# Modulation vectors after the first two chunks: products with a full row sum on TensorE, or scaling and summing on GpSimd with a last sum on TensorE

## The chip, the core and the metric

The kernel runs on one core of a Trainium2 chip. The core has TensorE (PE, matrix products into PSUM), VectorE (DVE), ScalarE (ACT) and GpSimd (POOL), each working through its own queue of instructions in order, and SyncE (SP), whose queue here issues the transfers of weights. ScalarE's queue issues transfers too. The metric is the device time of one execution in microseconds (us); a time of several executions is their median.

## What is computed

A block of two layers over 256 latent tokens and 256 context tokens with 1024 features. Each layer is modulated by six vectors of 1024 values for each of the two streams, cut from one product of a vector with a 1024 x 6144 matrix:

```python
c_act = jax.nn.silu(c)
cc_act = jax.nn.silu(c_ctx)
for l in range(DEPTH):
    sh1, sc1, g1, sh2, sc2, g2 = jnp.split((c_act @ w_mod[l] + b_mod[l])[:, None, :], 6, axis=-1)
    csh1, csc1, cg1, csh2, csc2, cg2 = jnp.split(cc_act @ w_mod[l] + b_mod[l], 6, axis=-1)
    y, yc = token_mixer(modulate(x, sh1, sc1), modulate(xc, csh1, csc1), ...)
    x = layer_norm(DEEPNORM_ALPHA * x + g1 * y, ln1_g[l], ln1_b[l])
    x = layer_norm(DEEPNORM_ALPHA * x + g2 * swiglu(modulate(x, sh2, sc2), ...), ln2_g[l], ln2_b[l])
    # the context stream the same with csh1 ... cg2, in the first layer only
```

`modulate` is a layer norm times (1 + scale) plus shift. The token mixer has a gated linear attention (GLA) with 4 heads, a differential attention with 8 heads and a latent attention (MLA) with 8 heads, merged by gates. The feed-forward part has 2816 hidden values. All inputs are float32.

## The kernel before

Weights come in tiles of up to 128 x 1024 values by a transfer on SP's queue into one of four buffers called raw (`load`, `fetch`, L181 to L196). Each half of a tile is split into a rounded part wh, by a copy on ScalarE (L212), and the rest wl, by a subtraction on VectorE (L213), and every product is made of three (`mm3`, L233): the lines L234, L235 and L236 are most of TensorE's work. Three tiles of wh and wl run ahead. The tile framework orders each engine's queue beforehand, by the priority that the order of the program gives and by what its plan takes for the times; on the chip each queue then runs strictly in that order.

The modulation vectors are made in pieces. Shift and scale of the first sub-layer of layer 0 are made at the start (`first_X`, `mod_first`, L277, closing product L318). All others stand in `mod_queue` (L334): four chunks of layer 0 and six of layer 1, each in two pieces of 512 columns, 20 pieces. A piece has four steps (`mod_step`, L289). A step loads 256 rows of 512 columns (L296) and makes eight small full-precision products (L299) whose stationary side is 32 columns of silu(c), two of them used; the four groups of 128 columns stand in four column groups of the array. After four steps ScalarE copies the sums (L304). `mod_close` (L309) brings them to columns by one product with a selector (L320), adds the bias (L325), halves the gates (L327), and, when a gate's chunk is whole, writes it to memory (L331) from 128 partitions, one value each. `gate_rows` (L354) later reads it back, spread over all partitions, by transfers on ScalarE's queue (L410).

What sets the place of the steps is `tick` (L338). It is called ahead of each weight tile, and every third call closes a finished piece and makes the next step. The last two pieces, the second gate of layer 1, are left out there; `mods_until` (L346) makes them in one go ahead of the last feed-forward part, and closes what is still open.

GpSimd does little: fills, and the power in `rpow` (L178), which every norm needs and which VectorE waits for (L702 and L795 in the heads, L381 in `modulate`), and a small product (L792). After the mixer, `load_cur` (L141, called at L1152) fetches the residual tokens on ScalarE's queue. The output projection keeps the last HELD column blocks of `w_out` from the first two token tiles for the other two (L1173).

Of the kernel before, what the change touches and what calls it, by code (L numbers as in the profile page):

```python
# [8 lines left out]
F32 = mybir.dt.float32  # L9
F32R = mybir.dt.float32r  # L10
AF = mybir.ActivationFunctionType
ALU = mybir.AluOpType
# [31 lines left out]
def hybrid_block_kernel(  # L44
# [18 lines left out]
    BUFS = dict(X=3, XL=3, A=3, Y=15, U=8, M=16, acc=8, a2r=2, a2=2, early=4, xt=2, raw0=11, raw1=5, u=27, wo=33, q=6, k=6, v=16, e=6, pT=11, rt=5, mr=3, mz=8, qr=2, rs=8, gt=6, o=3)  # L63
# [9 lines left out]
    HELD = 4  # L73
    FHELD = 1
    RND = 12
    PB = dict(mm=8, s=2, t=2, o=6, md=1, first=15)
# [13 lines left out]
    def keep(shape):  # L90
        """Columns of the store for what stays for the whole program."""
# [14 lines left out]
    def small(w=1):  # L106
        """w columns for values that are needed soon and briefly."""
        o = small_n[0]
        if o + w > SMALL:
            o = 0  # L110
        small_n[0] = o + w
        return ring[:, o:o + w]
# [8 lines left out]
    # the first transfers of a queue leave in the order given here  # L121
# [35 lines left out]
    # silu(c) and silu(c_ctx) as columns, the rest of the 32 columns zero  # L157
# [13 lines left out]

    mhalf = keep([P, 1])
    nc.gpsimd.memset(mhalf, -0.5)

    def rpow(o, v, a):
        """o = (v + a) ** -0.5 on a column."""
# [4 lines left out]
    def load(src, kt, n, tag=None):  # L181
        """[kt * 128, n] of a weight, at most 1024 values to a partition."""
# [5 lines left out]
    nfetch = [0]  # L188

    def fetch(raw, src, kt, n):  # L190
# [4 lines left out]
        nfetch[0] += 1  # L195
        return v  # L196

    def split(v, tag=None):
        """v [128, a, b] -> hi, lo as lists of a views [128, b]: products read them by k."""
# [21 lines left out]
    def wtiles(src, kt, cols):  # L221
        """Column ranges of a [kt * 128, .] weight side by side."""
# [15 lines left out]
    def feat_block(o, w, X, n0, n1, c0=0, m=P):  # L238
        """o[m, n] = sum_k w[k, c0:c0+m]^T X[k, n0:n1]"""
# [5 lines left out]
    def wfeat(src):  # L245
        """A [1024, 128] weight."""
# [3 lines left out]
    def wtok(src, tag=None):  # L250
        """A [1024, 256] weight as two halves of k."""
# [4 lines left out]
    def tok_block(o, ws, X, t0, c0, c1):  # L256
        """o[128 tokens, c1-c0] = X[:, t0:t0+128]^T w[:, c0:c1], k in order of ws"""
# [8 lines left out]
    # chunks of w_mod: 0 sh1, 1 sc1, 2 g1, 3 sh2, 4 sc2, 5 g2  # L266
# [5 lines left out]
    def mod_load(l, ch, pc, j, tag=None):  # L272
        """512 rows of 256 columns."""
# [3 lines left out]
    def mod_first(ch, pc, raws):  # L277
        """256 columns of a chunk of layer 0, both streams, by token; eight k tiles on four column groups."""
# [10 lines left out]
    def mod_step():  # L289
        """A quarter of a piece: 512 columns of a chunk, both streams, by token; each 128 have a column group."""  # L290
# [1023 lines left out]
```

## Time and profile before

| | before |
|---|---|
| device time, median of 3 runs | 2157.45 us (2156.32 to 2159.31) |
| span of the profiled execution, first to last instruction | 2154.1 us |
| TensorE busy | 2099.5 us, 97% |
| VectorE busy | 1436.7 us, 67% |
| ScalarE busy | 1076.6 us, 50% |
| GpSimd busy | 96.0 us, 4% |
| mean granted TensorE clock | 0.992 |

The span covers the profiled execution from its first to its last instruction; the times of the runs take in what lies around it as well. Busy times of TensorE (PE) are modelled at their ends, since its products overlap, so the distance from the start of one instruction to the start of the next is the better measure there. PEclk is the clock that TensorE was granted, as a part of full speed. A row of a group gives the line, the engine, the operation, the tiles written and read, the shapes and the number of instructions, then the busy time in us and the mean of one in ns, and then the engine's idle time ahead of them.

### The profile page before, as it was taken

The page shows a single profiled execution, that of the slowest core. Times are in us where ns is not written, and L with a number is a line of the kernel's source. Part 1 is how long each engine was busy: PE and PEld are TensorE (multiplying, and loading weights), DVE is VectorE, ACT ScalarE, POOL GpSimd, SP SyncE. Part 2 cuts the span into 40 slices and gives each one's busy share as a digit, 9 for nine tenths or more (in the row PEclk, how much of TensorE's full clock was granted, in tenths as well). Part 3 has the DMA queues.
Part 4 walks back from the last instruction along what each step waited for, and adds up shares of the span by engine and source line. Part 5 has one row for each costly group of instructions (what it writes and reads, how often), then busy time and mean ns, then how long its engine had stood idle before and what let it go on. Part 6 is the DMA issues. An engine that isn't in the chain of part 4 may idle for free.

```text
span 2154.1 us, 36382 instructions
## 1 busy us (share of the span) xinstructions
PE 2099.5 (97%) x14103; PEld 1812.2 (84%) x14103; DVE 1436.7 (67%) x3168; ACT 1076.6 (50%) x2495; POOL 96.0 (4%) x187
## 2 busy tenths in 40 slices
PE   7999999999999999999999999999999999998998
PEld 4888887777777778799899889988978888998998
DVE  5699657767467666685334448598566888785656
ACT  3756345666454553434231334765465676644452
POOL 0001001111000000010000000000000000000000
PEclk9999999999999999999999999999999999998999
DMA  9322343332322234627324446533434333568653
GB/s 294 102 87 69 118 99 93 86 106 60 91 81 66 78 127 137 176 84 214 104 89 127 118 127 182 159 91 118 136 88 128 106 113 85 172 191 213 172 178 116
DMA packets 349270, 268.29 MB, mean 125 GB/s; under 512 B 19932, under 2 KB 316520, under 8 KB 349096
## 3 DMA queue, kind: packets, MB, share of 16 engines
q1 hardware_dynamic: 335632, 252.22, 40.1%
q10 hardware_dynamic: 13464, 13.74, 2.1%
q8 instruction: 111, 1.82, 0.3%
q14 instruction: 63, 0.52, 0.1%
HBM read 263.79 MB, written 2.12 MB: 123 GB/s over the span
## 4 chain that ended last, share of the span: by engine, by line
PE 79%; DVE 11%; ACT 4%; issue 2%; POOL 2%; DMA 1%; ACTq 0%; DVEq 0%; POOLq 0%
PE ps_mm L234 18%; PE ps_mm L235 18%; PE ps_mm L236 18%; PE ps_s L234 3%; PE ps_s L236 3%; PE ps_s L235 3%; PE ps_s L509 3%; POOL store L178 2%; PE ps_s L508 2%; DVE wl L213 2%; PE ps_md L299 1%; PE ps_s L681 1%; DMA grow<-store 1%; ACT rt L483 1%; PE ps_t L928 1%
## 5 line engine op out<-in xcount | busy, mean ns | idle before, releaser
L213 DVE TENSOR_TENSOR wl<-raw,wh 128x512 fp32r<-128x512 f32 (+2 forms) x719 | 468.8, 674 | 139.7 <-ACT wh L212 82.4
L212 ACT CAST wh<-raw 128x512 fp32r<-128x512 f32 (+2 forms) x719 | 416.2, 611 | 254.1 <-PE ps_mm L235 135.0
L234 PE MATMUL ps_mm<-X,wh 128*128 128x512 f32 (+1 forms) x1264 | 440.8, 349 | 0.0
L235 PE MATMUL ps_mm<-XL,wh 128*128 128x512 f32 (+1 forms) x1264 | 437.4, 346 | 0.0
L236 PE MATMUL ps_mm<-X,wl 128*128 128x512 f32 (+1 forms) x1264 | 435.7, 345 | 0.0
L234 PEld LDWEIGHTS ps_mm<-X,wh 128*128 128x128 f32 x1264 | 241.2, 191 | 33.3 <-issue 7.3
L235 PEld LDWEIGHTS ps_mm<-XL,wh 128*128 128x128 f32 x1264 | 241.3, 191 | 27.3 <-issue 2.7
L236 PEld LDWEIGHTS ps_mm<-X,wl 128*128 128x128 f32 x1264 | 241.0, 191 | 26.2 <-issue 0.7
L236 PE MATMUL ps_mm<-wh,XL 128*128 128x256 f32 (+1 forms) x544 | 156.8, 292 | 0.0
L235 PE MATMUL ps_mm<-wl,X 128*128 128x256 f32 (+1 forms) x544 | 156.5, 292 | 0.1
L234 PE MATMUL ps_mm<-wh,X 128*128 128x256 f32 (+1 forms) x544 | 152.8, 294 | 0.0
L178 POOL TENSOR_TENSOR store<-store 128x1 f32<-128x1 f32 x112 | 75.6, 676 | 1657.4 <-DVE store L177 1633.9
L234 PE MATMUL ps_s<-X,wh 128*128 128x256 f32 (+1 forms) x384 | 126.2, 329 | 4.9 <-ACT wh L212 4.9
L236 PE MATMUL ps_mm<-wh,u 128*128 128x256 f32 x444 | 125.8, 283 | 0.0
L235 PE MATMUL ps_mm<-wl,u 128*128 128x256 f32 x444 | 125.6, 283 | 0.0
L234 PE MATMUL ps_mm<-wh,u 128*128 128x256 f32 x444 | 125.6, 283 | 0.0
L236 PE MATMUL ps_s<-X,wl 128*128 128x256 f32 (+1 forms) x384 | 125.1, 326 | 0.0
L235 PE MATMUL ps_s<-XL,wh 128*128 128x256 f32 (+1 forms) x384 | 125.0, 326 | 0.0
L234 PE MATMUL ps_mm<-Y,wh 128*128 128x512 f32 (+1 forms) x352 | 119.9, 341 | 0.1
L235 PE MATMUL ps_mm<-Y,wh 128*128 128x512 f32 (+1 forms) x352 | 118.6, 337 | 0.0
L236 PE MATMUL ps_mm<-Y,wl 128*128 128x512 f32 (+1 forms) x352 | 118.4, 336 | 0.0
L723 ACT ACTIVATE e<-ps_s,store 128x512 f32<-128x512 f32 (+1 forms) x144 | 88.5, 617 | 47.1 <-DVE store L721 45.4
(306 smaller groups left out, 4481.7 us busy)
## 6 DMA issues: line engine op xcount, KB each, us to landing
raw<-in_w_in_dram SPq DMA_DIRECT2D x144, 512.0 KB, 4.6
raw<-in_w_mod_dram SPq DMA_DIRECT2D x96, 512.0 KB, 3.7
raw<-in_ffn_w_in_dram SPq DMA_DIRECT2D x96, 512.0 KB, 7.1
raw<-in_w_branch_dram SPq DMA_DIRECT2D x48, 512.0 KB, 3.5
raw<-in_ffn_w_out_dram SPq DMA_DIRECT2D x46, 512.0 KB, 3.4
raw<-in_w_out_dram SPq DMA_DIRECT2D x16, 512.0 KB, 4.2
raw<-in_w_in_dram SPq DMA_DIRECT2D x16, 448.0 KB, 3.4
v<-grow ACTq DMA_DIRECT2D x12, 256.0 KB, 4.1
```

Source lines behind the costliest of these rows:

```text
L178: nc.gpsimd.tensor_tensor(o, o, mhalf, op=ALU.pow)
L212: nc.scalar.copy(h, v[:, o:o + step, :])
L213: tt(lo, v[:, o:o + step, :], r32(h), op=ALU.subtract)
L234: mm(o, lh, rh, start=start, stop=False)
L235: mm(o, lh, rl, start=False, stop=False)
L236: mm(o, ll, rh, start=False, stop=stop)
L299: mm(pm[32 * g:32 * g + 32, :], cst[:, 2 * j + k, :], v[:, k, P * g:P * g + P], start=(j == 0 and k == 0), stop=(j == 3 and k == 1))
L483: act(qw[a:a + 32, :], pl[b:b + 32, :], AF.Copy, scale=f)
L508: mm(o, qs[m][:, q], ks[m][:, k], start=start, stop=False)
L509: mm(o, qs[2][ROWS[m], q], ks[m][ROWS[m], k], start=False, stop=stop)
L681: mm(pa[:, i, :], kx[:, P * i:P * i + P], qx[:, P * j:P * j + P], start=True, stop=True)
L723: act(e, pscore, AF.Exp, bias=mx, accum_out=s)
```

## The change

The pieces in `mod_queue` are no longer multiplied on TensorE. `mod_step` loads the same rows into tiles of their own (mraw, three of them), placed on SP's queue behind the weight load last issued. For each of the two row tiles and each stream GpSimd scales the 128 x 512 weights by a column of silu(c) and adds the result to an accumulator (macc). Both streams are made only where both are used: in layer 0 and in the first two chunks of layer 1. `mod_close` then sums over partitions on TensorE. For shifts and scales that is a product of each 128 columns with a column of ones; for gates it is a product of a constant 128x128 tile of 0.5 with the 512 columns, whose first row, with half of the bias row (fetched on ScalarE's queue), is written to memory as one piece of 512 values. The PSUM bank of the old sums goes. Two more edits: HELD is 3 instead of 4, and the transfers of `load_cur` stand on ScalarE's queue behind the last rounding copy that the program issued ahead of the last gate blocks. In the diff, edits that take away comments alone are left out.

```diff
-    BUFS = dict(..., mr=3, ...)
+    BUFS = dict(..., mr=4, mraw=3, macc=6, mt=1, ...)
-    HELD = 4
+    HELD = 3
-    PB = dict(mm=8, s=2, t=2, o=6, md=1, first=15)
+    PB = dict(mm=8, s=2, t=2, o=6, first=15)
+    halves = keep([P, P])
+    nc.gpsimd.memset(halves, 0.5)
 def fetch(raw, src, kt, n):
...
+    seen["load"] = getattr(ins, "ins", ins)
 def mod_step():
+    l, ch, pc = mod_queue[0]
     if not mod_now:
-        mod_now.extend([0, ps("md", [P, P])])
-    j, pm = mod_now
-    l, ch, pc = mod_queue[0]
+        n = 2 if l < DEPTH - 1 or ch < 2 else 1
+        mod_now.extend([0, [T([P, 512], "macc") for _ in range(n)]])
+    j, sums = mod_now
     c0 = ch * D + 512 * pc
-    v = load(w_mod[l, 256 * j:256 * j + 256, c0:c0 + 512], 2, 512)
+    with tc.issue_after(seen["load"]):
+        v = load(w_mod[l, 256 * j:256 * j + 256, c0:c0 + 512], 2, 512, "mraw")
     for k in range(2):
-        for g in range(4):
-            mm(pm[32 * g:32 * g + 32, :], cst[:, 2 * j + k, :], v[:, k, P * g:P * g + P],
-               start=(j == 0 and k == 0), stop=(j == 3 and k == 1))
+        for s, a in enumerate(sums):
+            c, fresh = cst[:, 2 * j + k, s:s + 1], j == 0 and k == 0
+            t = a if fresh else v[:, k, :] if s == len(sums) - 1 else T([P, 512], "mt")
+            nc.gpsimd.tensor_scalar(t, v[:, k, :], c, None, op0=ALU.mult)
+            if not fresh:
+                nc.gpsimd.tensor_tensor(a, a, t, op=ALU.add)
     mod_now[0] += 1
     if j == 3:
-        row = T([P, 512], "mr")[:, 0:P]
-        nc.scalar.copy(row, pm)
-        mod_open.append((l, ch, 4 * pc, 4, row))
+        mod_open.append((l, ch, 4 * pc, 4, sums))
 def mod_close():
-    l, ch, k0, nk, row = mod_open.pop(0)
+    l, ch, k0, nk, sums = mod_open.pop(0)
+    if ch in (2, 5):
+        if (l, ch) not in grow:
+            grow[l, ch] = tc.dram_tile([2, D], F32, name=f"grow{l}_{ch}")
+        br = T([P, 512], "mr")[0:1, :]
+        nc.scalar.dma_start(br, b_mod[l:l + 1, ch * D + P * k0:ch * D + P * k0 + 512])
+        for s, a in enumerate(sums):
+            pt = ps("mm", [P, 512])
+            mm(pt, halves, a, start=True, stop=True)
+            row = T([P, 512], "mr")[0:1, :]
+            stt(row, br, 0.5, pt[0:1, :], op0=ALU.mult, op1=ALU.add)
+            nc.scalar.dma_start(grow[l, ch][s:s + 1, P * k0:P * k0 + 512], row)
+        return
...
-        mm(pt, row, sel[:, 2:10], start=True, stop=True)
+        ns = len(sums)
+        for q in range(nk):
+            for s, a in enumerate(sums):
+                mm(pt[:, ns * q + s:ns * q + s + 1], a[:, P * q:P * q + P], scan1[:, 0:1], start=True, stop=True)
...
-    if ch in (2, 5):
-        ts(o, o, 0.5, None, op0=ALU.mult)
-        if k0 + nk == KD:
-            d = tc.dram_tile([2, D], F32, name=f"grow{l}_{ch}")
-            for s in range(2 if l < DEPTH - 1 else 1):
-                nc.scalar.dma_start(d[s].rearrange("(k p) -> p k", p=P), mc[:, :, s])
-            grow[l, ch] = d
 def hilo(src, hi, lo, f=None):
     if f is None:
-        nc.scalar.copy(hi, src)
+        ins = nc.scalar.copy(hi, src)
+        seen["act"] = getattr(ins, "ins", ins)
...
+    heads_done = seen["act"]
     XM = [pair("M", TQ) for n in range(KD)]
     gates(2, range(8))
     G1, B1 = bcast_row(ln1_g[l], "e"), bcast_row(ln1_b[l], "e")
-    load_cur(NT)
+    with tc.issue_after(heads_done):
+        load_cur(NT)
```

## Rows read from the trace of the kernel before

**Rows 1.** The page: busy us, share of the span and instructions of each engine.

```profile
PE 2099.5 (97%) x14103; PEld 1812.2 (84%) x14103; DVE 1436.7 (67%) x3168; ACT 1076.6 (50%) x2495; POOL 96.0 (4%) x187
```

**Rows 2.** Busy time by stretch: from:to, length, each engine (instructions), PEclk, DMA share, GB/s.

```profile
323.10:646.20 323.10, 317.33 (x1797) 245.34 (x1797) 221.54 (x535) 187.68 (x504) 34.70 (x70) 1.00 0.29 86
861.60:915.50 53.90, 48.64 (x301) 40.98 (x299) 34.75 (x62) 23.26 (x42) 0.00 (x0) 0.94 0.65 176
107.70:215.40 107.70, 103.57 (x643) 88.23 (x642) 102.19 (x230) 62.40 (x138) 9.25 (x16) 1.00 0.25 78
1400.10:1454.00 53.90, 52.05 (x385) 47.44 (x385) 52.61 (x157) 33.31 (x89) 1.68 (x6) 1.00 0.32 91
1938.60:1992.50 53.90, 45.71 (x361) 43.98 (x361) 30.74 (x62) 22.80 (x51) 0.55 (x1) 0.84 0.89 213
```

**Rows 3.** Stretches again, the instructions of L299 alone: PE and PEld busy, PEclk, DMA.

```profile
107.70:215.40 107.70, 1.93 (x48) 1.13 (x48) 1.00 0.25 78
323.10:646.20 323.10, 11.23 (x224) 5.86 (x224) 1.00 0.29 86
1400.10:1454.00 53.90, 1.89 (x34) 1.08 (x34) 1.00 0.32 91
1930.00:1945.00 15.00, 3.91 (x118) 3.09 (x122) 0.91 0.65 189
```

**Rows 4.** Timeline of TensorE, four places: start us, us, line, tiles, count, [idle before].

```profile
18.23 0.61 PE L318 MATMUL ps_mm<-store,mr 128*128 128x2 f32 x4
...
221.71 0.39 PE L235 MATMUL ps_mm<-XL,wh 128*128 128x512 f32 x1
221.94 0.39 PE L236 MATMUL ps_mm<-X,wl 128*128 128x512 f32 x1
222.26 0.64 PE L299 MATMUL ps_md<-raw,store 128*32 128x128 f32 x16
222.83 0.50 PE L234 MATMUL ps_mm<-X,wh 128*128 128x512 f32 x1
...
882.63 0.28 PE L320 MATMUL ps_mm<-store,mr 128*128 128x8 f32 x2
882.84 0.64 PE L299 MATMUL ps_md<-raw,store 128*32 128x128 f32 x16
...
1963.55 0.58 PE L234 MATMUL ps_s<-X,wh 128*128 128x256 f32 x1 [2.96 <-ACT wh L212]
```

**Rows 5.** Groups of TensorE by line and shape: the closing products of the start.

```profile
L318 PE MATMUL ps_mm<-store,mr 128*128 128x2 f32 x32 | 4.6, 248 | 0.5 <-ACT mr L284 0.5
```

**Rows 6.** The chain that ended last, its longest pieces: start us, us, what.

```profile
253.18 1.73 PE ps_s L630 x8
...
1951.37 11.11 DMA grow<-store
```

**Rows 7.** Groups of GpSimd by line and shape.

```profile
L178 POOL TENSOR_TENSOR store<-store 128x1 f32<-128x1 f32 x112 | 75.6, 676 | 1657.4 <-DVE store L177 1633.9 <-DVE store L614 23.2
L792 POOL TENSOR_SCALAR store<-store 128x1 f32<-128x1 f32 x48 | 16.6, 345 | 301.7 <-ACT e L723 301.5
L525 POOL MEMSET a2r<- 96x512 f32 x4 | 2.0, 522 | 43.1 <-DVE XL L471 43.1
L155 POOL MEMSET store<- 128x256 f32 x1 | 0.3, 312 | 0.3 <-POOLq L1298 0.3
```

**Rows 8.** Timeline of VectorE and GpSimd at two places.

```profile
332.28 0.41 DVE L485 SCALAR_TENSOR_TENSOR rt<-ps_mm,store 128x256 f32<-128x256 f32 x1
...
332.44 0.55 POOL L178 TENSOR_TENSOR store<-store 128x1 f32<-128x1 f32 x1 [0.58 <-DVE store L177]
...
1578.10 0.68 DVE L213 TENSOR_TENSOR wl<-raw,wh 128x512 fp32r<-128x512 f32 x1
...
1578.26 0.93 POOL L178 TENSOR_TENSOR store<-store 128x1 f32<-128x1 f32 x1 [1.91 <-DVE store L177]
```

**Rows 9.** Waits of the whole span: who for whom, us in total, times, longest.

```profile
DVE o L795 <- POOL store L178: 13.2, 32, 0.7
```

More of the change, by code (lines that the diff above doesn't have):

```diff
@@ L61, in nm @@
         return f"{s}_{uid[0]}"
-    BUFS = dict(X=3, XL=3, A=3, Y=15, U=8, M=16, acc=8, a2r=2, a2=2, early=4, xt=2, raw0=11, raw1=5, u=27, wo=33, q=6, k=6, v=16, e=6, pT=11, rt=5, mr=3, mz=8, qr=2, rs=8, gt=6, o=3)
+    BUFS = dict(X=3, XL=3, A=3, Y=15, U=8, M=16, acc=8, a2r=2, a2=2, early=4, xt=2, raw0=11, raw1=5, u=27, wo=33, q=6, k=6, v=16, e=6, pT=11, rt=5, mr=4, mraw=3, macc=6, mt=1, mz=8, qr=2, rs=8, gt=6, o=3)
     def T(shape, tag, dtype=F32):
@@ L188, in hybrid_block_kernel @@
     nfetch = [0]
+    seen = {}
     def fetch(raw, src, kt, n):
@@ L314, in mod_close @@
         mc = mcols[l, ch]
+        ns = 2
         pt = ps("mm", [P, 2 * nk])
@@ L317, in mod_close @@
             for q in range(2):
-                mm(pt[:, 2 * q:2 * q + 2], row[:, P * q:P * q + P], sel[:, 0:2], start=True, stop=True)
+                mm(pt[:, 2 * q:2 * q + 2], sums[:, P * q:P * q + P], sel[:, 0:2], start=True, stop=True)
         else:
-            mm(pt, row, sel[:, 2:10], start=True, stop=True)
+            ns = len(sums)
+            for q in range(nk):
+                for s, a in enumerate(sums):
+                    mm(pt[:, ns * q + s:ns * q + s + 1], a[:, P * q:P * q + P], scan1[:, 0:1], start=True, stop=True)
         b0 = 48 * l + 8 * ch + k0
-        bias = bcol[:, b0:b0 + nk].rearrange("p (q o) -> p q o", o=1).to_broadcast([P, nk, 2])
-        o = mc[:, k0:k0 + nk, :]
-        p3 = pt.rearrange("p (q s) -> p q s", s=2)
-        stt(o, p3, 1.0 if ch in (1, 4) else 0.0, bias, op0=ALU.add, op1=ALU.add)
-        if ch in (2, 5):
-            ts(o, o, 0.5, None, op0=ALU.mult)
-            if k0 + nk == KD:
-                d = tc.dram_tile([2, D], F32, name=f"grow{l}_{ch}")
-                for s in range(2 if l < DEPTH - 1 else 1):
-                    nc.scalar.dma_start(d[s].rearrange("(k p) -> p k", p=P), mc[:, :, s])
-                grow[l, ch] = d
+        bias = bcol[:, b0:b0 + nk].rearrange("p (q o) -> p q o", o=1).to_broadcast([P, nk, ns])
+        p3 = pt[:, 0:ns * nk].rearrange("p (q s) -> p q s", s=ns)
+        stt(mc[:, k0:k0 + nk, 0:ns], p3, 1.0 if ch in (1, 4) else 0.0, bias, op0=ALU.add, op1=ALU.add)
     mod_queue = [(l, ch, pc) for l in range(DEPTH) for ch in range(6) for pc in range(2) if l or ch > 1]
```

## The prediction

> **What bounds the kernel now.** I read the busy totals of the page first: TensorE is busy 97% of the span, VectorE 67%, ScalarE 50%, GpSimd 4% [rows 1]. So whatever leaves TensorE's stream is time, as long as nothing else takes its place, and GpSimd has room. Then I split the span into stretches [rows 2]. Three kinds of stretch matter. In the first GLA heads of layer 0 (107.7 to 215.4 us) VectorE is busy 102.2 of 107.7 us and TensorE 103.6: both are full. At the start of layer 1's GLA heads (1400.1 to 1454.0) VectorE is busy 52.6 of 53.9. In the differential-attention part of layer 0 (323.1 to 646.2) VectorE has 101 us idle. Two stretches, around 890 and 1960 us, have an idle TensorE and a granted clock of 0.94 and 0.84; what stops it there is told below. The stretches by the line of the old modulation products, L299, show where a quarter-piece ("step") falls: 16 instructions are one step, so 48, 224, 34 and 118 instructions are 3, 14, about 2 and about 7 steps [rows 3].
>
> **What is taken off TensorE.** 20 pieces of four steps make 80 steps; a step is 16 instructions of L299 [rows 4]. One step starts at 222.26 us and the next product at 222.83: 0.57 us. The product ahead of it lasted 0.32 us to the step's start, where an ordinary one takes 0.23 (221.71 to 221.94), so another 0.09 [rows 4]. 80 x 0.66 = 53 us. The closing product L320 takes 882.63 to 882.84, 0.21 us [rows 4], 20 x 0.21 = 4 us. Together 57 us. Seven of the steps run from 1930 to 1945 us [rows 3], a burst while TensorE waits for the residual and layer norm anyway; 7 x 0.66 = 5 us of it is no gain. Gain: 52 us.
>
> **What is put on TensorE.** A close of a shift or scale piece now takes one full-precision product with a 128x128 stationary and a single moving column for each 128 columns and stream: 8 pieces with two streams (8 products each) and 4 with one (4 products), 80 products. A product is two instructions, as L318 shows: four of them take 0.61 us, and one alone 0.248, so (0.61 - 0.25) / 3 = 0.12 us from start to start [rows 4, 5]. 80 x 2 x 0.12 = 19 us. A close of a gate piece is one product of 512 moving columns for each stream: 4 pieces with two and 4 with one, 12 products, 24 instructions. Eight instructions of 256 columns take 1.73 us [rows 6], 0.216 each, so 0.43 for 512: 24 x 0.43 = 10 us. Added: 29 us. Net off TensorE: 52 - 29 = 23 us.
>
> **The gate rows' way through memory.** Today a finished gate chunk is written as single elements from 128 partitions (L331), and the write takes 11.1 us at 1951.37 [rows 6]; one more such write stands in the chain, as long, in the stretch from 861.6 us. ScalarE's queue holds the read of it (L410) next, so ScalarE stops, then the weight casts, then TensorE. For the later one that is 2.96 us of TensorE's waiting [rows 4], and a share of the clock: the stretch has 8.2 us of idle TensorE, and its clock of 0.84 (a part of it at the lower level, 1.2 GHz) costs 0.16 x 53.9 = 8.6 us [rows 2]; 2.96 of 8.2 idle makes 3.1 of it. For the earlier one, TensorE is idle 53.9 - 48.6 = 5.3 us, and 0.06 of 53.9 us, 3.2 us, goes with the clock [rows 2]. The new rows are written as 2 KB in one piece by partition 0. If ScalarE no longer stops there, 6.1 + 8.5 = 14.6 us come back; bounds 0 (the row now comes later and stops the same queue) and 15. I take 14: nothing else of the chain in those stretches is as long as the write. So the two gains make 37 us.
>
> **What GpSimd now does.** 12 pieces with two streams have 16 scalings and 14 sums, 8 with one stream half that: 256 scalings and 224 sums of 128x512. The trace has no such operation, only narrow ones and fills. A fill of 512 columns takes 0.522 us and one of 256 takes 0.312 [rows 7], 0.82 ns a column. A scaling of one column takes 0.345 us [rows 7]; with 511 more columns 0.345 + 0.42 = 0.76. A sum reads two operands: 0.76 if side by side, 0.345 + 0.84 = 1.18 if in turn, 0.676 + 0.84 = 1.51 at L178's base [rows 7]. I take 1.18, the middle. A step with two streams is 4 x 0.76 + 4 x 1.18 = 7.8 us, with one 3.9; in all 256 x 0.76 + 224 x 1.18 = 459 us, 21% of the span. A close comes a tick later: three weight loads of 24 products at 0.23 us, 16 us, in layer 0 and half that in layer 1. So in the ticked stretches sums are in time and TensorE doesn't wait; in a backlog it could, 0 to 30 us (the last burst's 8 steps x 3.9), taken as 0. The Trainium skill ("GPSIMD Engine Reference", section "Performance versus the Vector engine") gives about 2.6 cycles per element for a two-input operation on GpSimd; by it a sum would take about 1.1 us, an estimate, and the total 441 us; no run here has yet shown one.
>
> **What that costs beside it.** First the read port. L178 takes 0.55 us when VectorE is at L485, which reads PSUM and one operand of SBUF, but 0.93 when L213, with two SBUF operands, is running: it ends 0.41 us after L213 does [rows 8]. So GpSimd waits out a VectorE instruction of two SBUF operands. The other direction, VectorE waiting for a wide GpSimd operation, has no row, since GpSimd's reads are one column today. The bounds are 0 and the whole read, 0.42 us for a scaling and 0.84 for a sum: 5.0 us a step with two streams, 2.5 with one, 256 x 0.42 + 224 x 0.84 = 296 us in all. I take the whole read, times the chance that VectorE wants the port. The Trainium skill ("SBUF — State Buffer", section "Who interferes with whom") calls it an exclusive lock, held for the whole instruction, the later one blocked; for GpSimd as the later one the trace agrees (0.93 against 0.55).
> In the first GLA stretch, 3 steps x 5.0 x 0.9 = 13.5 us less 5.5 idle is 8 us; at 1400 us, 2 x 2.5 x 0.95 = 4.8 less 1.3 is 3. In the differential heads 14 x 5.0 = 70 us, half of it met, 35 us against 101 us of idle VectorE; as it falls in chains of softmax and norm, I take a quarter, 9 us (0 to 35). In the feed-forward parts it is hidden by VectorE's idle time: 0.
> Second, the power L178 now queues behind modulation on GpSimd; VectorE's L795, L702 and L381 wait for it, and behind them on VectorE stand the weight splits L213. Today that wait is 13.2 us in 32 times at L795 [rows 9]. GpSimd would be busy 14 x 7.8 = 109 of 323 us, a chance of 0.34; 40 powers x 0.34 x 0.9 us (one operation on average) = 12 us, a quarter of it on the path, 3, and 1 in layer 1 (0 to 16). Third, the residual stage at 1930 to 1945: three powers and the two-operand L984 beside the last burst, 3 us (0 to 12). Fourth, HELD 3 loads and splits one w_out block again: 4 x 0.68 us (L213 [rows 8]) on VectorE, 1 us (0 to 3).
> Edits at no cost: loads of w_mod queue on SP behind the last weight load and wait there for GpSimd to free one of three tiles, so weight loads stand behind them; the four weight buffers cover that, which w_mod no longer shares. If GpSimd falls a whole step behind, 7.8 us, cover is gone and ScalarE's casts and TensorE wait for the rest. The late load_cur on ScalarE's queue is hidden by eight gate blocks, 8 x 24 x 0.23 = 44 us. The fill of the new constant lies in the start.
> Sum of the costs: 11 + 9 + 4 + 3 + 1 = 28 us.
>
> **How the numbers follow.** 2154.1 - 37 + 28 = 2145.1 us of span. The median of the runs, 2157.45, is 3.35 above the span, so 2148.5 us, 0.4% faster. A difference under 0.2%, 4.3 us, can hardly be told from none.
> Forecast, gain partly eaten, 2130 to 2153 us: chance 0.33.
> Rival A, VectorE's idle time hides nearly all: costs of 5 to 9 us, 2157.45 - 37 + 8 = 2128, down to 2115 if the free weight buffers give TensorE a little more. For it: VectorE is idle for a third of the span [rows 1]. Chance 0.16.
> Rival B, no change: costs of 33 to 41 us, or TensorE's columns go but its operands come no sooner (the change doesn't do what it says; only the gate rows' 14 us are left against some 12 of cost): 2153 to 2161. Chance 0.14.
> Rival C, slower: the port. VectorE's two-operand instructions wait for GpSimd's reads in the attention heads as well, and the in-order VectorE hands that on to the weight splits and the softmax. It decides when more than 37 of the 296 us, one eighth, reach the end; at a fifth, 59 us, it is 2157.45 - 37 + 59 = 2179, at a quarter 2194. For it: [rows 8] and a full VectorE in the GLA stretches; against it: the idle third elsewhere, and the feed-forward parts, which take their share of the steps. Chance 0.37. By the Trainium skill's lock ("SBUF — State Buffer", same section) this is the rival to expect when both engines are busy; its mechanism here is worked out above from rows.
> Faster 0.33 + 0.16 = 0.49, same 0.14, slower 0.37. The range of 2115 to 2194 takes in A, the forecast, B and C up to a quarter; the forecast's own is 2130 to 2153.
>
> **What would show it.** Right: L299 gone, the closes near 29 us, no wait for a grow write over 3 us, GpSimd busy 450 to 600 us with sums near 1.2 us. Right on the port: L213 longer than 0.68 us beside a wide GpSimd operation, and more VectorE time in the GLA stretches. Wrong: waits of TensorE on GpSimd at the closes, waits of VectorE on L178 far over 20 us, or SP waiting for GpSimd ahead of weight loads; then C's price is too low.

## The result and the profile after

The change makes the kernel slower: 2341.38 us (median of 4 runs, 2334.76 to 2345.84) against 2157.07 us in the same session, a ratio of 1.0853 with an interval of 1.084 to 1.0865. The forecast was 2148.5 us, the range ended at 2194. The profiled execution of after has a span of 2341.9 us, 188 us above the one of before.

The page first: its span, and busy us, share and instructions by engine (compare [rows 1]).

```profile
span 2341.9 us, 35242 instructions
PE 2124.9 (91%) x12967; PEld 1835.0 (78%) x12967; DVE 1589.1 (68%) x3168; ACT 1104.1 (47%) x2479; POOL 865.6 (37%) x668
```

TensorE has 1136 products fewer and is busy longer. GpSimd went from 96 to 866 us, and VectorE, which has the same number of instructions, from 1437 to 1589: the same work takes it 152 us more.

Where the time went is read best by stage. I cut each trace at the same products: the first of the GLA heads, the first scores of the differential heads, the last transposition of these heads, the first product with w_out, the first with w_ffn_out's operand (`ps_mm<-wh,u`), the last of layer 0's `ps_mm<-wo,u` (the stage called norms begins there), and so on for layer 1. The lengths, in us, with the experiments told below:

| stage | before | after | norms off GpSimd | scaling on ScalarE | sums filled | fills | narrow |
|---|---|---|---|---|---|---|---|
| start | 66.9 | 68.1 | 72.8 | 70.8 | 69.8 | 82.2 | 69.0 |
| GLA heads, layer 0 | 248.1 | 278.5 | 277.8 | 272.0 | 264.7 | 248.9 | 249.5 |
| differential heads, layer 0 | 302.8 | 373.8 | 307.4 | 313.3 | 340.0 | 305.3 | 306.4 |
| MLA heads and gates, layer 0 | 277.3 | 296.1 | 297.0 | 282.9 | 321.9 | 290.2 | 285.6 |
| w_out, residual, first feed-forward, layer 0 | 202.8 | 220.6 | 196.4 | 205.6 | 216.9 | 187.3 | 182.9 |
| feed-forward, layer 0 | 219.8 | 216.5 | 216.5 | 216.5 | 216.6 | 216.6 | 216.5 |
| norms to layer 1 | 59.4 | 64.9 | 63.0 | 68.2 | 65.2 | 59.1 | 59.1 |
| GLA heads, layer 1 | 188.8 | 206.4 | 197.4 | 198.3 | 190.9 | 185.4 | 185.5 |
| differential heads, layer 1 | 206.9 | 212.6 | 210.8 | 213.0 | 211.7 | 207.6 | 207.4 |
| MLA heads, layer 1 | 137.5 | 139.4 | 138.9 | 139.4 | 139.4 | 138.9 | 138.9 |
| w_out, residual, first feed-forward, layer 1 | 172.7 | 194.0 | 195.6 | 178.9 | 188.4 | 176.2 | 169.3 |
| feed-forward, layer 1 | 71.1 | 71.0 | 71.2 | 71.1 | 71.1 | 71.1 | 71.2 |

The feed-forward part of layer 0 is the only stage that gained (3.3 us). The largest loss, 71 us, is in the differential heads of layer 0, then 30 us in its GLA heads, 18 to 21 us in each of four others. Here are the first two, before and then after, and three others of after (columns as in [rows 2]).

```profile
66.90:315.00 248.10, 243.86 (x1542) 209.67 (x1540) 191.17 (x395) 141.11 (x295) 11.57 (x22) 1.00 0.32 94
315.00:617.80 302.80, 297.03 (x1688) 227.16 (x1687) 207.52 (x508) 174.27 (x480) 35.75 (x72) 1.00 0.31 89
```

```profile
68.10:346.60 278.50, 250.74 (x1384) 213.08 (x1385) 225.37 (x395) 142.48 (x295) 143.27 (x105) 0.96 0.26 77
346.60:720.40 373.80, 315.03 (x1504) 242.01 (x1503) 222.80 (x509) 176.43 (x478) 180.43 (x170) 0.90 0.24 71
1016.50:1237.10 220.60, 191.98 (x1189) 175.54 (x1188) 131.98 (x233) 71.42 (x141) 148.87 (x96) 0.93 0.38 114
1237.10:1453.60 216.50, 216.50 (x1374) 197.21 (x1373) 112.09 (x189) 63.69 (x106) 47.79 (x32) 1.00 0.39 121
2076.90:2270.90 194.00, 161.69 (x1271) 157.89 (x1271) 123.81 (x229) 78.11 (x161) 51.58 (x34) 0.90 0.56 161
```

The two stages lose in different ways. In the GLA heads VectorE runs the same 395 instructions for 225.4 instead of 191.2 us: 34 us more, against 30 us of stage. In the differential heads VectorE grows by only 15 us, but the stage by 71: TensorE stands idle for 373.8 - 315.0 = 58.8 us where it was 5.8. The granted clock is 0.90 there, some of it at the lower of the two levels (1.2 GHz), after stretches in which TensorE was idle. Its 1504 products take 315 us; the 1504 of the kernel called narrow below take 291.9 us at 1.00, so the clock costs about 23 us on top of the waits.

GpSimd's groups (form of [rows 7]) show what the added operations cost.

```profile
L308 POOL TENSOR_SCALAR mraw<-mraw,store 128x512 f32<-128x512 f32 x140 | 261.1, 1868 | 138.7 <-DMA mraw<-in_w_mod_dram 138.3 <-DVE rt L1177 0.3
L310 POOL TENSOR_TENSOR macc<-macc,mraw 128x512 f32<-128x512 f32 x140 | 190.3, 1359 | 6.2
L308 POOL TENSOR_SCALAR mt<-mraw,store 128x512 f32<-128x512 f32 x84 | 153.0, 1822 | 292.8 <-DMA mraw<-in_w_mod_dram 256.8 <-PE ps_mm L239 35.8
L310 POOL TENSOR_TENSOR macc<-macc,mt 128x512 f32<-128x512 f32 x84 | 118.3, 1409 | 3.8
L180 POOL TENSOR_TENSOR store<-store 128x1 f32<-128x1 f32 x112 | 73.5, 658 | 542.0 <-DVE store L179 535.0 <-DVE store L631 6.7
L308 POOL TENSOR_SCALAR macc<-mraw,store 128x512 f32<-128x512 f32 x32 | 58.0, 1820 | 315.8 <-DVE wo L217 145.4 <-DMA mraw<-in_w_mod_dram 125.1 <-DVE U L981 33.1
```

A scaling (L308) takes 1.82 to 1.87 us on the mean, a sum (L310) 1.36 to 1.41; together 780.7 us. Undisturbed they take 1.56 and 1.26 us, about the shortest of the trace. The row of L180 has the other half of the story: GpSimd sat idle for 535 us waiting for VectorE to hand it the input of a power, with its next scalings queued behind.

The waits of after, engine by engine (form of [rows 9]), have VectorE waiting for those same powers.

```profile
DVE o L812 <- POOL store L180: 44.1, 37, 5.2
DVE rs L850 <- POOL store L180: 30.4, 11, 7.4
DVE A L1002 <- POOL store L180: 19.7, 3, 10.7
DVE q L397 <- POOL store L180: 16.6, 8, 7.3
DVE o L719 <- POOL store L180: 16.2, 22, 3.8
...
PE ps_t L400 <- DVE q L397: 37.1, 10, 12.4
PE ps_t L815 <- DVE o L812: 24.4, 24, 3.8
PE ps_mm L327 <- POOL macc L310: 15.3, 1, 15.3
...
SPq L195 <- POOL macc L310: 40.6, 6, 17.6
```

L812 is the old L795: 44.1 us where [rows 9] has 13.2. All five come to 127 us, where all such waits of before come to 27. TensorE then waits for what VectorE does next (L815, L400).

One such wait, from the timeline of after, first GpSimd, then VectorE, then TensorE.

```profile
565.96 1.29 POOL L310 TENSOR_TENSOR macc<-macc,mraw 128x512 f32<-128x512 f32 x1
567.21 1.27 POOL L310 TENSOR_TENSOR macc<-macc,mt 128x512 f32<-128x512 f32 x1
568.45 1.56 POOL L308 TENSOR_SCALAR mraw<-mraw,store 128x512 f32<-128x512 f32 x1
570.10 1.26 POOL L310 TENSOR_TENSOR macc<-macc,mraw 128x512 f32<-128x512 f32 x1
571.32 0.57 POOL L180 TENSOR_TENSOR store<-store 128x1 f32<-128x1 f32 x1
...
566.15 0.21 DVE L179 TENSOR_SCALAR store<-store 128x1 f32<-128x1 f32 x1
...
571.92 0.35 DVE L812 TENSOR_SCALAR o<-ps_o,store 128x128 f32<-128x128 f32 x1 [5.22 <-POOL store L180]
572.19 0.47 DVE L798 SCALAR_TENSOR_TENSOR e<-e,store,e 128x256 f32<-128x256 f32 x1
...
572.72 0.69 PE L749 MATMUL ps_t<-store,e 128*128 128x128 f32 x2 [5.02 <-DVE e L798]
```

VectorE gave the input of the power at 566.36. GpSimd had four wide operations ahead of it in its order, the first of them running, and came to it at 571.32. VectorE, in order too, had L798 behind L812, and TensorE waited 5.02 us for L798.

The other way of losing, from the GLA heads of after: sums on GpSimd beside VectorE. Then one scaling of the last burst.

```profile
106.11 1.43 POOL L310 TENSOR_TENSOR macc<-macc,mraw 128x512 f32<-128x512 f32 x1
107.50 1.72 POOL L310 TENSOR_TENSOR macc<-macc,mt 128x512 f32<-128x512 f32 x1
...
106.33 1.75 DVE L217 TENSOR_TENSOR wl<-raw,wh 128x512 fp32r<-128x512 f32 x1
108.00 1.49 DVE L680 TENSOR_TENSOR pT<-mz 128x256 f32<-128x256 f32 x1
...
2081.79 5.09 POOL L308 TENSOR_SCALAR macc<-mraw,store 128x512 f32<-128x512 f32 x1 [145.36 <-DVE wo L217]
```

The split L217 is the old L213, 0.68 us in [rows 8]; here it takes 1.75 us, and L680 beside the second sum 1.49 us, where the same instruction takes 0.41 at 102.25 us. In the last line it is GpSimd that suffers: while VectorE runs nine instructions, most with two operands in SBUF, one scaling takes 5.09 instead of 1.56 us.

### The profile page after: what moved, and what is told of

The parts are those of the page before. It is cut to its first block, busy times and chain, and to the rows that moved or that the text cites. A ratio compares the mean times of both kernels' runs of the same rounds, so it can differ in the third digit from the quotient of the medians.

```text
span 2341.9 us, 35242 instructions
## 1 busy us (share of the span) xinstructions
PE 2124.9 (91%) x12967; PEld 1835.0 (78%) x12967; DVE 1589.1 (68%) x3168; ACT 1104.1 (47%) x2479; POOL 865.6 (37%) x668
## 5 line engine op out<-in xcount | busy, mean ns | idle before, releaser
L217 DVE TENSOR_TENSOR wl<-raw,wh 128x512 fp32r<-128x512 f32 (+2 forms) x727 | 541.3, 750 | 374.6 <-PE ps_mm L240 144.0
L216 ACT CAST wh<-raw 128x512 fp32r<-128x512 f32 (+2 forms) x727 | 439.8, 611 | 576.9 <-PE ps_mm L239 266.9
L238 PE MATMUL ps_mm<-X,wh 128*128 128x512 f32 (+1 forms) x1264 | 448.9, 355 | 2.9 <-ACT k L595 1.7
L239 PE MATMUL ps_mm<-XL,wh 128*128 128x512 f32 (+1 forms) x1264 | 444.9, 352 | 2.2 <-DVE XL L409 2.2
L240 PE MATMUL ps_mm<-X,wl 128*128 128x512 f32 (+1 forms) x1264 | 442.9, 350 | 1.7 <-DVE wl L217 1.7
L308 POOL TENSOR_SCALAR mraw<-mraw,store 128x512 f32<-128x512 f32 x140 | 261.1, 1868 | 138.7 <-DMA mraw<-in_w_mod_dram 138.3
L180 POOL TENSOR_TENSOR store<-store 128x1 f32<-128x1 f32 x112 | 73.5, 658 | 542.0 <-DVE store L179 535.0
L308 POOL TENSOR_SCALAR mt<-mraw,store 128x512 f32<-128x512 f32 x84 | 153.0, 1822 | 292.8 <-DMA mraw<-in_w_mod_dram 256.8
L310 POOL TENSOR_TENSOR macc<-macc,mraw 128x512 f32<-128x512 f32 x140 | 190.3, 1359 | 6.2
L308 POOL TENSOR_SCALAR macc<-mraw,store 128x512 f32<-128x512 f32 x32 | 58.0, 1820 | 315.8 <-DVE wo L217 145.4
L239 PE MATMUL ps_mm<-wl,X 128*128 128x256 f32 (+1 forms) x544 | 163.2, 302 | 11.0 <-DVE wl L217 11.0
```

The lines of the kernel that those rows point to most:

```text
L180: nc.gpsimd.tensor_tensor(o, o, mhalf, op=ALU.pow)
L216: nc.scalar.copy(h, v[:, o:o + step, :])
L217: tt(lo, v[:, o:o + step, :], r32(h), op=ALU.subtract)
L238: mm(o, lh, rh, start=start, stop=False)
L239: mm(o, lh, rl, start=False, stop=False)
L240: mm(o, ll, rh, start=False, stop=stop)
```

## The experiments

All ratios are to the kernel before, measured beside each. HELD 2 in place of 3 gives the edited kernels the room in SBUF that they need; the first run shows what that alone does.

**The changed kernel with HELD 2.**

```diff
-    HELD = 3
+    HELD = 2
```

> The changed kernel with HELD 2 instead of 3 and nothing else: one more w_out block is loaded and split again. It is the control for the next three runs, which need the room. Every theory expects the changed kernel's own time within 1%: 2320 to 2365 us. If it is far off, w_out's blocks matter more than the 1 us that the prediction took.

Measured: 2338.19 us, ratio 1.0829 (1.0798 to 1.0861). It is the changed kernel for all that follows.

**The powers off GpSimd.** The queue behind which they stood is taken away, the port is left.

```diff
-        nc.gpsimd.tensor_tensor(o, o, mhalf, op=ALU.pow)
+        nc.vector.reciprocal(o, o)
...
-            nc.gpsimd.memset(cb[:, o:o + 1], 0.0)
+            nc.vector.memset(cb[:, o:o + 1], 0.0)
...
-                nc.gpsimd.tensor_scalar(g0, s0, s0, 128.0 * EPS, op0=ALU.mult, op1=ALU.mult)
+                nc.vector.tensor_scalar(g0, s0, s0, 128.0 * EPS, op0=ALU.mult, op1=ALU.mult)
```

> The changed kernel with HELD 2, and everything small taken off GpSimd: the power of the norms becomes a reciprocal on VectorE (the root is left out, so norms are not the reference's), the small product and the fills of the heads go to VectorE as well. GpSimd then does modulation alone, and nothing that VectorE waits for stands in its queue, closes excepted. Theory queue (VectorE stops behind powers that stand behind wide operations on GpSimd; these waits went from some 27 to some 127 us): most of the loss goes, 2200 to 2260 us. Theory port (VectorE's two-operand instructions are blocked by GpSimd's reads, 126 us longer in sum than before): little goes, 2300 us or more. Theory late closes (TensorE stands at a close until the sums are there): little goes, 2300 us or more.

Measured: 2245.66 us, ratio 1.0401 (1.037 to 1.0431). 92 of the 179 us are gone. Its stretches, GLA and differential heads of layer 0 (columns as above):

```profile
72.80:350.60 277.80, 248.22 (x1378) 212.35 (x1378) 225.05 (x419) 142.70 (x295) 139.01 (x81) 0.96 0.26 77
350.60:658.00 307.40, 291.87 (x1505) 225.65 (x1504) 239.41 (x581) 174.21 (x477) 152.58 (x98) 1.00 0.30 86
```

The differential heads are back at 307.4 us with the clock at 1.00, although VectorE works more than in after (239 us). So nearly all of their 71 us comes only with the powers in GpSimd's queue. The GLA heads stay at 277.8 us: there it isn't the queue.

**Fills in place of scalings and sums.** GpSimd is held about as long, but reads nothing. A fill into an accumulator or into mt does not wait for loaded weights either, so it can run earlier than the operation that it replaces.

```diff
-                nc.gpsimd.tensor_scalar(t, v[:, k, :], c, None, op0=ALU.mult)
+                nc.gpsimd.memset(t.bitcast(mybir.dt.uint8)[:, 0:1792], 0)
...
-                    nc.gpsimd.tensor_tensor(a, a, t, op=ALU.add)
+                    nc.gpsimd.memset(a.bitcast(mybir.dt.uint8)[:, 0:1408], 0)
+                else:
+                    nc.gpsimd.memset(a[:, 448:512], 0.0)
```

> The changed kernel with HELD 2, and each scaling and each sum replaced by a fill of bytes (1792 and 1408) that takes about as long, with the same writes but no read of SBUF: the modulation vectors are not computed. The queue of GpSimd stays as long as the fills last, the read port is free. Theory port: VectorE's instructions are back at their times of before, and most of the loss goes, 2200 to 2260 us. Theory queue: the powers still wait, 2290 us or more, if a fill lasts about 1.5 us; in proportion less if it is shorter. Theory late closes: as theory queue.

Measured: 2178.73 us, ratio 1.0097 (1.0081 to 1.0113), with a GpSimd busy for 770.0 us. The split of the weights, fills first, then the same group of after and of before:

```profile
L217 DVE TENSOR_TENSOR wl<-raw,wh 128x512 fp32r<-128x512 f32 x679 | 461.9, 688 | 330.5 <-PE ps_mm L240 103.8 <-issue 68.2 <-PE ps_mm L239 55.2
```

```profile
L217 DVE TENSOR_TENSOR wl<-raw,wh 128x512 fp32r<-128x512 f32 x671 | 508.3, 763 | 345.1 <-PE ps_mm L240 135.4 <-PE ps_mm L239 70.8 <-PE ps_s L240 59.8
```

```profile
L213 DVE TENSOR_TENSOR wl<-raw,wh 128x512 fp32r<-128x512 f32 x663 | 440.5, 686 | 113.6 <-ACT wh L212 66.3 <-PE ps_mm L236 21.2 <-issue 18.2
```

Beside fills it takes 688 ns as in before, beside scalings and sums 763. So it is reading, not being busy, that lengthens this split. 13 of the 32 us that fills has over narrow are in the start, where VectorE's busy time too is 13 us longer: a thing of the fills (below).

**Both at once.**

```diff
 the edits of the last two kernels, and macc=4 in place of 6
```

> Both edits of the two runs before at once: the norms' power (as a reciprocal, so norms are not the reference's) and small work on VectorE, and GpSimd's scalings and sums as fills (the modulation vectors are not computed); HELD 2, and 4 accumulators instead of 6 for room. With norms_off_gpsimd (2246 us), fills (2179) and held2 (2338) it makes a square of queue and port. If the port alone costs what norms_off_gpsimd still loses, the time is that of narrow, 2140 to 2165 us, and the port's price without any queue is some 90 us. If late closes or the burst make the rest, it stays at 2200 us or more. If queue and port simply add, 2179 - 92 = 2087 us, less than the kernel can give by the sum of its products: so they share waits, and 2140 or more is to be expected by every theory that has a shared path.

Measured: 2180.08 us, ratio 1.0094 (1.0074 to 1.0115). The four kernels make a square. By the medians, the powers' place on GpSimd costs 2338 - 2246 = 92 us with reads and nothing without (2179 against 2180). But the start of this last kernel is spoilt by the fills. A row of them, which waits for nothing, keeps GpSimd busy from 2.3 to 55.0 us; a small VectorE instruction does not end until the row has, and TensorE waits behind it (one line of the timeline, one of the waits).

```profile
8.82 46.25 DVE L166 TENSOR_SCALAR store<-store 128x16 f32<-128x16 f32 x1
...
PE ps_t L467 <- DVE store L179: 48.5, 1, 48.5
```

Its first product of the GLA heads comes at 119.3 us, where held2 has it at 68.7, and the two others at 72.8 and 82.2. From that product to the end, the profiled executions take, in us:

| | powers on GpSimd | powers on VectorE |
|---|---|---|
| scalings and sums | 2268.3 | 2172.0 |
| fills | 2086.6 | 2059.4 |

So behind the start the powers' place costs 96 us beside scalings and sums, and 27 beside fills (35 by the median of fills, which is 8 us above its profiled run). Scalings and sums cost 113 us over fills with the powers away, and 182 with them there. Each costs something alone, and the queue about three times as much where GpSimd and VectorE hold each other up. What the fills change is not the reading alone: in fills at most two wide operations stood ahead of a power whose input was ready, in held2 up to eleven.

**The norms moved in the kernel before.** The same three edits, without the change.

> The kernel before with the same edit of the norms (reciprocal on VectorE instead of the power on GpSimd, small product and fills on VectorE; norms are not the reference's). It is the control for norms_off_gpsimd: what the shorter way of the norms is worth without modulation on GpSimd. VectorE's 27 us of waits for the power go at most, a third of it on the path by the prediction's reckoning: 2140 to 2155 us. Well under 2130 would mean that most of the 92 us of norms_off_gpsimd is not from the queue behind modulation.

Measured: 2164.95 us, ratio 1.0027 (1.0017 to 1.0037): 6 us slower. The 92 us are not a gain that the moved norms would bring to any kernel.

**Narrow operations.** All instructions, loads, waits and closes of the change stay, GpSimd's wide ones work on 8 columns.

```diff
-                nc.gpsimd.tensor_scalar(t, v[:, k, :], c, None, op0=ALU.mult)
+                if fresh:
+                    nc.gpsimd.memset(a, 0.0)
+                nc.gpsimd.tensor_scalar(t[:, 0:8], v[:, k, 0:8], c, None, op0=ALU.mult)
...
-                    nc.gpsimd.tensor_tensor(a, a, t, op=ALU.add)
+                    nc.gpsimd.tensor_tensor(a[:, 0:8], a[:, 0:8], t[:, 0:8], op=ALU.add)
```

> The changed kernel with HELD 2, and each scaling and each sum cut to 8 of its 512 columns (an accumulator is filled with zeros first), so the modulation vectors are not computed: the same instructions in number and order of dependencies, but each short. Queue, port and lateness go together. If the prediction's gains hold (23 us of products, 14 us of the gate rows' way), 2110 to 2135 us. If the other edits (HELD, load_cur, the separate load tiles, another plan of the queues) cost something of their own, it stays at 2150 us or more.

Measured: 2147.22 us, ratio 0.994 (0.9918 to 0.9963), GpSimd busy 306.0 us. This is what the change would be worth if GpSimd's width were nearly free: 12 us. And 2338 - 2147 = 191 us is the price of the width.

**The side edits alone**, on the kernel before: HELD 3 and the later transfers of the tokens.

```diff
-    HELD = 4
+    HELD = 3
...
+        heads_done = seen["act"]
-        load_cur(NT)
+        with tc.issue_after(heads_done):
+            load_cur(NT)
```

> The kernel before with HELD 3 and the late load_cur alone; modulation stays on TensorE. By the prediction 1 us of splits and nothing for load_cur: 0.998 to 1.003 of the time of before. Over 1.005 would mean that the side edits carry a part of the loss.

Measured: 2170.79 us, ratio 1.0047 (1.003 to 1.0064). **HELD 3 alone**, the first two lines of that diff:

> The kernel before with HELD 3 in place of 4 and nothing else; with the later load of the current tokens it was 0.47% slower (11 us). Theory: a cast held back one step less costs it, the whole 11 us are here: about 2168 to 2171. Rival: the later load (moved behind the heads of the layer) costs it, HELD costs 0 to 1 us: 2157 to 2160.

Measured: 2166.63 us, ratio 1.0031 (1.002 to 1.0043). So HELD makes 7 of the 10 us. In the first layer it only moves work (13.6 us more in the MLA stage, 12.5 less in the next). The loss is in layer 1, 5.8 us in the GLA heads and 3.8 in the differential heads; what in them is slower I have not found.

**The gate rows alone**, on the kernel before: TensorE keeps the modulation sums, but a finished gate piece goes to memory in rows of 128 values from four partitions; four small products add the bias in PSUM, and ScalarE's copy halves.

```diff
+            if gate:
+                for g in range(4):
+                    r = 48 * l + 8 * ch + 4 * pc + g
+                    e = ident[0:48 * DEPTH, r:r + 1].to_broadcast([48 * DEPTH, 32])
+                    mm(pm[32 * g:32 * g + 32, :], e, b_rows, start=False, stop=True)
+                act(row, pm, AF.Copy, scale=0.5)
...
+            for s in range(2 if l < DEPTH - 1 else 1):
+                d = grow[l, ch][s, P * k0:P * k0 + 512].rearrange("(g c) -> g c", c=P)
+                nc.scalar.dma_start(d, row.rearrange("(g r) c -> g r c", r=32)[:, s, :])
+            return
```

> The kernel before with the gate rows' new way alone: modulation stays on TensorE; of a gate piece the bias is added to the sums by four small products, ScalarE halves them in its copy, and the row is written to memory in pieces of 128 values from four partitions, straight from the row tile, so the closing product, its VectorE work and the write of single values go. By the prediction 14 us (0.9935 of before, 2143 us), if ScalarE's stops behind the write of single values are the cause. If the write is slow for another cause, or ScalarE waits for the read all the same, no change, 0.998 or more.

Measured: 2147.76 us, ratio 0.9945 (0.993 to 0.996), faster than both kernels. Its two stretches from w_out to the feed-forward part, against 202.8 and 172.7 us before:

```profile
898.30:1094.00 195.70, 194.22 (x1387) 173.23 (x1384) 115.79 (x236) 72.14 (x149) 6.55 (x8) 1.00 0.48 138
1909.40:2074.20 164.80, 160.08 (x1410) 157.74 (x1409) 113.18 (x228) 75.71 (x163) 3.18 (x4) 0.98 0.69 194
```

7.1 and 7.9 us come back there, with the clock at 1.00 and 0.98.

**No burst at the end.** The last two pieces are made at ticks too.

```diff
-            if mod_queue and (mod_now or mod_queue[0] < (DEPTH - 1, 5, 0)):
+            if mod_queue:
```

> The changed kernel with HELD 2 and with the last two pieces of the queue read, scaled and summed at ticks like all others, so that nothing is left to be done in one go before the last residual stage. Theory of the late burst: the stalls at its end (12.5 us at 2098, 15.3 and 3.9 us at 2117 to 2134) go and nothing comes in their place: 2338 - 28 = about 2310. Rival, a wait that only moves: GpSimd has no time left between ticks either, the same two pieces (some 2 x 25 us of GpSimd work) delay the differential heads of the last layer instead, and the time stays within 8 us of 2338.

Measured: 2322.11 us, ratio 1.0752 (1.0737 to 1.0767). The two stages of layer 1 that matter, differential heads and residual:

```profile
1708.20:1940.00 231.80, 209.72 (x1260) 174.92 (x1259) 168.79 (x360) 138.58 (x348) 87.46 (x83) 0.95 0.35 105
2080.30:2245.40 165.10, 155.69 (x1266) 154.29 (x1265) 116.45 (x227) 77.60 (x161) 3.18 (x4) 0.97 0.59 163
```

Both theories are half right. The residual stage falls from 194 to 165.1 us, by 29 us, as expected. But the same work costs 19 us in the differential heads, 231.8 instead of 212.6.

**The scalings on ScalarE**, the sums on GpSimd as before.

```diff
-                nc.gpsimd.tensor_scalar(t, v[:, k, :], c, None, op0=ALU.mult)
+                nc.scalar.mul(t, v[:, k, :], c)
```

> The changed kernel with HELD 2; the 256 scalings run on ScalarE (a copy of the same shape there takes 611 ns: 157 us more on an engine that is busy for 47%), GpSimd keeps the 224 sums alone (1.29 us each, 289 us; after: 781 us of both). Theory of the port: the 159 us by which the changed kernel lies above its copy with fills go with the time in which GpSimd reads, 289 of 781: 59 us remain; what the fills cost by GpSimd's time alone (31 us between fills, busy for 770, and narrow, busy for 306) is nearly gone. Together 2147 + 59 = about 2206. Rival, GpSimd's time and queue alone: as narrow, with as little on GpSimd, 2147 to 2155. Second rival, ScalarE's own queue, in which the scalings now stand ahead of casts that TensorE waits for, 256 x 0.61 us, half of them on the path: 78 us more, about 2285.

Measured: 2232.58 us, ratio 1.0333 (1.0319 to 1.0347), between the theories. Its page and sums:

```profile
PE 2096.2 (94%) x12967; PEld 1812.4 (81%) x12967; DVE 1587.6 (71%) x3172; ACT 1254.5 (56%) x2739; POOL 427.3 (19%) x412
...
DVE o L812 <- POOL store L180: 15.0, 35, 1.3
```

VectorE is busy for 1587.6 us, as long as in after, though GpSimd's wide time has more than halved. So it is the sums that lengthen VectorE; the scalings do little. But without the scalings the powers come in time: L812 waits 15.0 instead of 44.1 us.

**The sums filled, the scalings kept**, the counterpart.

```diff
-                    nc.gpsimd.tensor_tensor(a, a, t, op=ALU.add)
+                    nc.gpsimd.memset(a.bitcast(mybir.dt.uint8)[:, 0:1408], 0)
```

> The changed kernel with HELD 2; the 256 scalings stay as they are (they read one wide operand), the 224 sums are replaced by fills of about the sums' length (1.28 us; they read nothing, so nothing is summed). Theory, the sums hold VectorE up: its busy time falls from 1589 to about 1490 us, as with fills alone (1489.4), a low product's cast beside a scaling takes 690 ns, and the time falls to 2180 plus what the scalings lose: they still stretch to up to 5 us when VectorE reads two operands, in the queue ahead of the powers: 2180 to 2230. Rival, every read of GpSimd holds VectorE up: 473 of 781 us of the reads remain, VectorE stays at about 1550 us, and 2179 + 0.6 x 159 = about 2275.

Measured: 2294.52 us, ratio 1.0616 (1.0594 to 1.0638), above both expectations, and VectorE busy for 1542.7 us. My theory was too simple. Two things stand in its trace. First, VectorE's waits for powers come to 108 us, near the 127 of after, and its 0.69 us split beside a scaling keeps a median of 0.69. Second, some 40 us of its time is of its own making:

```profile
852.69 15.84 POOL L310 MEMSET macc<- 128x1408 uint8 x13
...
852.15 16.91 DVE L937 TENSOR_SCALAR e<-e,store 128x512 f32<-128x512 f32 x2
```

```profile
DVE o L812 <- POOL store L180: 36.1, 35, 4.7
DVE A L1002 <- POOL store L180: 21.0, 5, 5.9
DVE o L719 <- POOL store L180: 20.6, 23, 4.5
DVE q L397 <- POOL store L180: 17.9, 7, 5.9
DVE rs L850 <- POOL store L180: 12.3, 10, 2.4
```

While GpSimd makes 13 fills in a row, a scaling of VectorE that takes 0.48 us elsewhere doesn't end until they have. Against held2, L937 is busy 28 us longer and L397 11, nearly all of it in four such waits, and TensorE waits 29 us for what L937 writes. Less these 40 us, if all of them lie on the path, the kernel would stand near 2255: some 76 us over fills, for the scalings alone. The sums alone cost 85 us over narrow, with ScalarE's added work in it. Both are worked out, not run, and since they are counted from different kernels they can't simply be added to the 159 us between fills and the changed kernel.

## Why the prediction was wrong, point by point

**What bounds the kernel.** "Whatever leaves TensorE's stream is time" held only in part. In the feed-forward part of layer 0 the seven steps and two closes gave 3.3 us in narrow, fills and after alike, near the 2.3 us that the terms give for that stage. In the attention heads of layer 0 it failed: by the same terms 24 steps less their closes were worth some 8 us; narrow is 1.4 and 3.6 us longer than before in those two stages. TensorE is 97% busy there, but its operands come from chains through VectorE, ScalarE and the norms, which the removed products were not part of.

**Off and on TensorE.** The sizes were right. The old products took 56.4 and 4.4 us from start to start (57 predicted for both). The new ones, in after (form of [rows 5]):

```profile
L344 PE MATMUL ps_mm<-store,macc 128*128 128x1 f32 x160 | 18.5, 244 | 0.0
L327 PE MATMUL ps_mm<-macc,store 128*128 128x512 f32 x24 | 12.6, 637 | 15.3 <-POOL macc L310 15.3
```

From start to start the 160 make 16.9 us (19 predicted), the 24 make 9.7 (10 predicted) without the waits in the last burst, of 15.3 and 3.3 us.

**The gate rows.** Right: 14 us predicted; the two stages gave 7.1 + 7.9 = 15.0 in the profile of gate_rows_alone, its median is some 11.5 us below. No wait for such a write is left among those of after.

**GpSimd's durations.** The sum was sized well, 1.18 against 1.26 us undisturbed. The scaling was not: 0.76 against 1.56. I put the fill's 0.82 ns a column under the one-column scaling [rows 7]; the real slope is (1.56 - 0.345) / 511 = 2.4 ns, and no row bounded it from above. The total is 781 us, not 459. The Trainium skill ("GPSIMD Engine Reference", section "Performance versus the Vector engine") has about 2.6 cycles per element for a sum, from which the prediction estimated 1.1 us; the trace has 1.26, some 15% more.

**The port.** The direction was right, the place half right. In the GLA heads of layer 0 I took 8 us, from three steps between 107.7 and 215.4 us; the whole stage has ten steps, and VectorE's added 34 us landed in full: 30 us. In layer 1 I took 3; 17.6 were lost, 21 against narrow. In the differential heads I took 9, and with the powers away they lose 4.6 (1.0 against narrow): no more than I took. The MLA heads and the first residual stage of layer 0 had no such term; in after the two are 36.6 us longer. With the powers away the kernel is still 98 us above narrow, most of it in the GLA heads (28 and 12 us), these two stages (11 and 14) and the last residual stage (26), so the port, with the late closes below, was sized several times too low.

**The queue behind which powers stand.** This is the step that failed by the largest factor. I took 3 + 1 us, at most 16, from one wide operation ahead of a power, a chance of 0.34 and a quarter on the path. In after 30 of the 112 powers had wide operations ahead of them when their input was ready, so the chance was about right. But there were up to nine of them, and they kept GpSimd busy for 128 us, 4.3 us for each such power and not 0.9. VectorE waits 127 us in all. Taking the powers away brings back 92 us, 63 of them in the differential heads of layer 0 (370.3 us in held2). The mistake was to treat the wait as a chance meeting. Both queues are in order and feed each other: GpSimd waits for VectorE's L179 (535 us), its scalings pile up behind the power, and the next power then stands behind the pile. The clock, which I had charged only to today's stalls, adds to each wait of TensorE.

**Late closes** were "taken as 0" out of 0 to 30 us. The last burst cost 29 us in its stage; one product of L327 waited 15.3 us for it. Taken away, it gave 16 us net, since its work then delays other stages. The last residual stage as a whole, put at 3 us (0 to 12), is 21 us longer in after.

**HELD and the later transfers** were put at 1 us and nothing; they cost 10 us on the kernel before, 7 with HELD alone. The 3 us between the two lie within their intervals, so "hidden by eight gate blocks" may stand.

**The cover of the weight buffers** held: SP's queue waited 40.6 us for GpSimd (longest 17.6), and the longest wait of TensorE for a weight's transfer is one of 0.3 us, in the start.

**The rivals.** Rival C, the port, is what happened. It was given 0.37 and ended at a quarter of 296 us. The wide operations of 781 us and what the powers make of them come to 191 us (narrow to the changed kernel), two and a half times that end. Its price counted VectorE's holding alone; the hand-on through GpSimd's queue was a term of the same mechanism, and multiplied it.

**What stays open.** The order of each queue is made beforehand, from what the plan takes for each operation, and it differs between kernels. Fills does 226 of its 770 us on GpSimd in the GLA heads of layer 0, after 143 of 866. What part of the 92 us is a plan that places wide operations ahead of powers, and what part is the length that reads add on the chip, was not separated. Nor was the port from the waits for loaded weights, which the fills mostly lack too.

## What to carry to other kernels

Before work is moved to an engine that is 4% busy, ask what short operations others wait for on it. A wide operation put ahead of them in an in-order queue is not paid in its own time but in the waits of every engine that comes back to it. Price an added operation by a row of the same operation and width, and where none exists, give the price the bound that the missing row leaves open. And take the harmless half of a change by itself: the gate rows alone, with nothing moved to GpSimd, make the kernel 0.55% faster.

## What the runs showed of the hardware

- On GpSimd a scaling with one wide operand (128x512 float32, 1.56 us) is slower than a sum of two (1.26 us).
- The two hold VectorE up differently. In after, a 128x512 split on VectorE takes 0.69 us (median) with nothing wide beside it, 0.69 beside a scaling and 1.42 beside a sum for at least half of its time (means 0.69, 0.77 and 1.30); a scaling, in turn, takes up to 5.9 us beside VectorE. What came first does not decide it: 111 splits that began while a scaling was running took 0.69, 51 that began while a sum was running 1.57 (medians). Beside fills the split takes 0.69. The Trainium skill ("SBUF — State Buffer", section "Who interferes with whom") says that a VectorE instruction with two inputs in SBUF contends with a GpSimd instruction that reads, not with one that only writes: fills agrees, and of the two that read the sums do; beside scalings it is mostly the scaling that gets longer.
- A row of 13 fills held one VectorE instruction with one operand in SBUF up for 16 us, and the row at the start of the kernel with both edits held a scaling of 16 columns up for 46 us. The same section of the Trainium skill has whoever comes second blocked until the first has finished; here it was blocked until a whole row of them had.
